# Two more block tiles for each feed-forward, with the norm's row multiplied in after the products

## The chip, the core and the metric

The kernel runs on one NeuronCore of a Trainium2 chip. The metric is the device time of one launch in microseconds (us), the median of several runs. The engines that matter are TensorE (PE, matmuls and, beside them, weight loads), VectorE (DVE), ScalarE (ACT), GpSimd (POOL, here a queue for DMAs that add into DRAM) and SyncE (SP, the queue that loads weights). Each engine executes its instructions in the order in which they were issued to it; an instruction that waits for another engine holds up everything behind it on its own engine.

## The reference

Two layers of a streaming encoder: 512 tokens, 1024 channels, float32. Each layer is a mixer and then a gated feed-forward with a causal convolution; the change lies in the feed-forwards alone.

```python
D_FF = ((8 * D_MODEL // 3 + 127) // 128) * 128          # 2816 = 22 tiles of 128
def rmsnorm(x, g):
    y = x32 * lax.rsqrt(jnp.mean(x32 * x32, axis=-1, keepdims=True) + EPS)
    return (y * g.astype(jnp.float32)).astype(x.dtype)
def conv_ffn(h, w_up, conv_w, conv_b, w_down):
    u, g = jnp.split(h @ w_up, 2, axis=-1)
    g = causal_dwconv(g, conv_w, conv_b)                # width 3
    return (jax.nn.silu(g) * u) @ w_down
x = x + conv_ffn(rmsnorm(x, norm_ffn_g[l]), ffn_w_up[l], ffn_conv_w[l], ffn_conv_b[l], ffn_w_down[l])
```

## The kernel before

**Layout.** Activations lie transposed: eight tiles `xT[j]` of 128 channels x 512 tokens. The factor of the norm is one number per token, the same for all channels; the kernel keeps it as a tile `norm.row` (128 x 512, all rows alike). Since it depends on the token alone, it may be multiplied in before the up-projection or on its result. The gain `g` is per channel and must be multiplied in before.

**Float32 products.** A float32 operand is split into a high and a low part (`split`, L138 to L141: ACT casts the high part, DVE subtracts for the low part), and a product is three matmuls (`mm3`, L194 to L196): high x high, high x low, low x high. So every weight tile costs a cast on ACT (`wh`, L140) and a subtraction on DVE (`wl`, L141) before PE can use it.

**The end of a mixer** (`finish`, L709). For each j the output projection `o` is added to `xT[j]` (L714), its square goes into the norm's sum (L288 on ACT, L289 on DVE), and `scaled` makes the high and low parts of x times g (L329 on ACT, L330 on DVE). The last three `o` are projected here, 24 matmuls of 512 columns each.

**The feed-forward's 22 tiles** of 128 hidden channels are made in two ways. A *plain* tile is two projections (gate, up) of 24 matmuls with 512 columns. A *block* tile handles the two projections and the two halves of the tokens as a 2 x 2 block product with seven products in place of eight: seven times 12 matmuls of 256 columns. For it, DVE forms sums of weights (L944) and the results are put together from the seven products (L890, L898 copies on ACT; L901, L910, L994 additions on DVE). The input side needs sums of x blocks too (`self.sums`, L807 and following splits); these are made once a layer.

Before, tiles 0 to 4 are plain and 5 to 21 are blocks. Plain tiles 0 to 2 use x times g, and the row is multiplied in afterwards (L774, L780). Beside them `forms` (L789) makes x times g times row, splits it into `ready` and forms the block sums from it; tiles 3 and 4 and all blocks use `ready`, so their results need no row.

**A block step** (`step`, L882) runs in an order written out by hand on PE, ACT and DVE. PE: product 1 (a11), 2 (a12), 3 (s2), 4 (s1), 5 (s3), the down products, product 6 (a22), 7 (s4). Products 1, 3, 5 and 6 accumulate in one PSUM bank `r1`, and ACT copies the bank between them: after product 1 (L898), after 3, 5 and 6 (L890). A later product into the bank cannot start before the copy of the earlier one is done. Between these, the step finishes the tile before it (`Tail`: last block, three taps of the convolution, Silu, product of gate and up, split), and prepares the weights of the tile after it (`nxt`). Outside the block steps a planner sets the order on each engine.

**The down-projection** of the first 16 hidden tiles is done in pieces beside the block tiles: a *unit* multiplies a group of k tiles with 128 output columns, ACT copies the result out of PSUM (L833), and a DMA on POOL's queue adds it into `xspill` in DRAM (L834). Two PSUM banks (`tr`) serve the units. Before, there are four groups of four k tiles, two units for each weight load.

Of the kernel before, what the change touches and what calls it, by code (L numbers as in the profile page):

```python
# [16 lines left out]
P = 128  # L17
# [37 lines left out]
def trunk(  # L55
# [632 lines left out]
    class OutProjection:  # L688
# [19 lines left out]
        def finish(self, gnames):  # L708
            logarithms()  # L709
            norm = Norm()  # L710
            acts = [[] for _ in gnames]
            for j in range(KT):
                o = self.o[j] if j in self.o else run(project(self.w, j * P, self.mixes))
                V.tensor_add(xT[j], xT[j], o)  # L714
                pin(G.dma_start(xspill[j], xT[j]))
                norm.add(xT[j])
                for a, g in zip(acts, gnames):
                    a.append(scaled(xT[j], g[:, j : j + 1]))
            return norm, acts

    class ChannelMixer:
# [9 lines left out]
        def __init__(self, l, act, norm, gain, beside):  # L731
            self.l, self.act, self.norm, self.gain, self.beside = l, act, norm, gain, beside
            self.w, self.fw, self.fb = ffn_w_up[l], col[f"fw{l}"], col[f"fb{l}"]
            self.hid, self.ready, self.down = [], [], {}
# [22 lines left out]
        def plain(self, j):  # L757
            scale = self.norm.row if j < UNSCALED else None
            act = self.act if j < UNSCALED else self.ready
            gate = project(self.w, DFF + j * P, act)  # L760
            up = project(self.w, j * P, act, "sc")
            if self.norm.row is None:
# [3 lines left out]
                scale = self.norm.row  # L766
# [3 lines left out]
            acc = sb("t", [P, S])  # L770
            src = og
            if scale is not None:
                src = sb("t", [P, S])
                V.tensor_tensor(out=src, in0=og, in1=scale, op=ALU.mult)  # L774
# [4 lines left out]
            if scale is not None:  # L779
                V.tensor_mul(acc, acc, scale)  # L780
# [5 lines left out]
        def forms(self):  # L786

            for j in range(KT):
                V.scalar_tensor_tensor(  # L789
                    xT[j], xT[j], self.gain[:, j : j + 1], self.norm.row, op0=ALU.mult, op1=ALU.mult  # L790
                )
                hi, lo = sb("u", [P, S], F32R), sb("u", [P, S], F32R)
                split(hi, lo, xT[j])
                self.ready.append((hi, lo))
                yield
            self.sums = []
            for k in range(KT // 2):
                b1, b2 = xT[k], xT[k + KT // 2]
# [18 lines left out]
        def load_down(self, q):  # L817

            g, jj = divmod(q, KT // 2)
            return load(rows(ffn_w_down[self.l], 2 * jj * P, 2 * P, GROUP * g, GROUP * (g + 1)), GROUP, 2 * P)  # L820

        def down_products(self, u):
            g, j = divmod(u, KT)
            w = self.down[u // 2]
            o = ps("tr")
            c = slice(u % 2 * P, (u % 2 + 1) * P)
            for k in range(GROUP):
                mm3(o, w[0][:, k, c], w[1][:, k, c], *self.hid[GROUP * g + k], k == 0, k == GROUP - 1)
            return j, o

        def add(self, j, o):
            t = sb("t", [P, S])
# [20 lines left out]
        def b(self, i, t):  # L853
            n = KT // 2
            return [tuple(x[:, t * H : (t + 1) * H] for x in p) for p in self.ready[i * n : (i + 1) * n]]
# [5 lines left out]
        def later(self):  # L861
# [17 lines left out]
            for part in (tail.last_block, tail.first_tap, tail.second_tap, tail.third_tap, tail.gated, tail.split):  # L879
                part()  # L880

        def step(self, j, w, nxt, tail):  # L882
# [10 lines left out]
            then(tail, "last_block", "first_tap")  # L893
# [17 lines left out]
            w.down_products(0)  # L911
            w.down_products(1)
# [5 lines left out]
            sum_products(new.pre[:, :H], r1, w.a22, 4)  # L918
            self.products(new.r3, w.s4, self.b(1, 1))
            return new, nxt  # L920

    class Forms:


        def __init__(self, mixer, j):
            self.mixer = mixer
            self.units = UNITS.get(j, (None, None))
            self.up, self.gate = mixer.load_pair(j)
            self.o = {}
            self.raw_down = {u // 2: mixer.load_down(u // 2) for u in self.units if u is not None and u % 2 == 0}  # L930
# [47 lines left out]
        def down_products(self, i):  # L978
            if self.units[i] is not None:
                self.o[i] = self.mixer.down_products(self.units[i])  # L980

        def add_down(self, i):
            if self.units[i] is not None:
                self.mixer.add(*self.o[i])

    class Tail:
# [5 lines left out]
        def last_block(self):  # L992
            c = self.up[:, H:]
            V.tensor_tensor(out=c, in0=c, in1=self.r3[:, :H], op=ALU.add)  # L994

# [18 lines left out]
    def channel_mixer(l, act, norm, gain, beside):  # L1014

        mixer = ChannelMixer(l, act, norm, gain, beside)
        forms = mixer.forms()
        run(mixer.plain(0))
        skips = -(turn[0] + 1) % 3
        for j in range(1, UNSCALED):  # L1020
            turn[0] += j <= skips
            weave(mixer.plain(j), forms, KT / (16.0 * (UNSCALED - 1)))
        until(lambda: len(mixer.ready) == KT, forms)
        mixer.buffers()
        for j in range(UNSCALED, PLAIN):
            units = UNITS.get(j, ())
            raws = {u // 2: mixer.load_down(u // 2) for u in units[::2]}
# [570 lines left out]
```

## Time and profile before

| | us |
|---|---|
| median of 3 runs | 1178.65 |
| lowest, highest | 1177.98, 1178.71 |
| span of the profiled execution (first to last instruction) | 1177.3 |
| PE busy | 1167.7 (99%) |
| DVE busy | 940.7 (80%) |
| ACT busy | 728.5 (62%) |

The profiled execution's time is known by its span alone. The stages of layer 0's feed-forward in it: the mixer's end from 253.8 us, plain tiles until about 340, block steps until about 580. Layer 1's: from 809 us, until about 894, until about 1136. In a timeline row stand the start, the duration, engine, line, operation and tiles, and in brackets the engine's idle time before the row and what ended it. A PE row's duration is modelled and overlaps the next; the distance of starts tells the rate.

### The profile page before, as it was taken

To read this page: it belongs to the slowest core of one execution; us is meant where nothing else is said; L and a number is where in the kernel's file an instruction comes from. 1 tells how busy PE (TensorE), PEld (TensorE's weight loads), DVE (VectorE), ACT (ScalarE), POOL (GpSimd) and SP (SyncE) were. 2 spreads that over 40 slices of the span, in tenths; PEclk is the share of its full clock that TensorE was granted. 3 is DMA by queue.
4 is the path that set the end of the run, shared out by engine and by line. 5 is a ranking of instruction groups with operands and counts; after the bars stand their busy time and mean duration, and the time that the engine had idled before them with its cause. 6 is when DMAs were issued, how large, how long until landed. Compare 5 with 4: busy or idle time off the path is not lost.

```text
span 1177.3 us, 18645 instructions
## 1 busy us (share of the span) xinstructions
PE 1167.7 (99%) x7005; PEld 1033.3 (88%) x7005; DVE 940.7 (80%) x1680; ACT 728.5 (62%) x1297; POOL 129.2 (11%) x222
## 2 busy tenths in 40 slices
PE   9999999999999999999999999999999999999997
PEld 9988888888889999999888888778889999999986
DVE  6777788887979888777688888897897887777755
ACT  6548677655656655666666677676565666666545
POOL 1211101000021111111020000101001011110100
PEclk9999999999999999999999999999999999999999
DMA  8645325243366766665563312335426456666551
GB/s 277 230 111 140 86 55 152 76 144 116 90 159 159 181 166 165 167 147 118 154 204 117 90 54 89 112 89 179 142 90 152 108 138 142 143 144 144 126 161 72
DMA packets 199277, 158.64 MB, mean 135 GB/s; under 512 B 8361, under 2 KB 178063, under 8 KB 199187
## 3 DMA queue, kind: packets, MB, share of 16 engines
q1 hardware_dynamic: 183026, 119.74, 34.5%
q0 software_dynamic: 15584, 36.67, 15.6%
q8 instruction: 55, 0.90, 0.3%
q10 hardware_dynamic: 576, 1.05, 0.2%
q14 instruction: 36, 0.29, 0.1%
HBM read 128.89 MB, written 32.46 MB: 137 GB/s over the span
## 4 chain that ended last, share of the span: by engine, by line
PE 95%; ACT 2%; DVE 2%; issue 0%; POOL 0%; POOLq 0%; DVEq 0%; ACTq 0%
PE pmm L194 18%; PE pmm L195 18%; PE pmm L196 18%; PE ptr L195 6%; PE ptr L194 6%; PE ptr L196 6%; PE psc L196 5%; PE psc L195 5%; PE psc L194 5%; PE psc L600 2%; PE ptr L1421 1%; PE ptr L1442 1%; PE ptr L1443 1%; PE ptr L669 0%; PE pmm L491 0%; PE pmm L470 0%
## 5 line engine op out<-in xcount | busy, mean ns | idle before, releaser
L194 PE MATMUL pmm<-u,wh 128*128 128x512 f32 (+1 forms) x968 | 333.2, 345 | 0.2 <-ACT u L140 0.2
L196 PE MATMUL pmm<-u,wl 128*128 128x512 f32 (+1 forms) x968 | 330.6, 342 | 0.0
L195 PE MATMUL pmm<-u,wh 128*128 128x512 f32 (+1 forms) x968 | 330.4, 342 | 0.0
L141 DVE TENSOR_TENSOR wl<-wr,wh 128x1024 fp32r<-128x1024 f32 (+3 forms) x172 | 199.7, 1162 | 82.4 <-ACT wh L140 80.9
L140 ACT CAST wh<-wr 128x1024 fp32r<-128x1024 f32 (+3 forms) x172 | 171.9, 1002 | 91.5 <-PE pmm L195 41.0
L196 PEld LDWEIGHTS pmm<-u,wl 128*128 128x128 f32 x968 | 181.8, 188 | 20.8
L194 PEld LDWEIGHTS pmm<-u,wh 128*128 128x128 f32 x968 | 181.8, 188 | 18.5 <-ACT u L140 1.1
L195 PEld LDWEIGHTS pmm<-u,wh 128*128 128x128 f32 x968 | 182.0, 188 | 18.1 <-DVE u L141 0.5
L194 PE MATMUL ptr<-u,wh 128*128 128x512 f32 x272 | 106.4, 391 | 0.0
L195 PE MATMUL ptr<-u,wh 128*128 128x512 f32 x272 | 106.2, 390 | 0.0
L196 PE MATMUL ptr<-u,wl 128*128 128x512 f32 x272 | 105.8, 389 | 0.0
L834 POOL DMA_DIRECT2D xspill<-t x64 | 55.5, 867 | 429.7 <-ACT t L833 417.2
L890 ACT COPY t<-pmm 128x256 f32<-128x256 f32 x102 | 38.0, 372 | 76.7 <-PE pmm L196 76.5
L141 DVE TENSOR_TENSOR u<-t,u 128x512 fp32r<-128x512 f32 (+1 forms) x94 | 54.1, 596 | 35.4 <-ACT u L140 35.4
L194 PE MATMUL pmm<-u,fh 128*128 128x256 f32 x272 | 75.4, 277 | 0.0
L194 PE MATMUL psc<-u,wh 128*128 128x256 f32 (+1 forms) x232 | 75.3, 324 | 0.0
L195 PE MATMUL pmm<-u,fh 128*128 128x256 f32 x272 | 75.2, 276 | 0.0
L196 PE MATMUL pmm<-u,fl 128*128 128x256 f32 x272 | 75.1, 276 | 0.0
L196 PE MATMUL psc<-u,wl 128*128 128x256 f32 (+1 forms) x232 | 75.1, 324 | 0.0
L195 PE MATMUL psc<-u,wh 128*128 128x256 f32 (+1 forms) x232 | 74.9, 323 | 0.0
L141 DVE TENSOR_TENSOR fl<-pt,fh 128x512 fp32r<-128x512 f32 x102 | 70.3, 689 | 5.1 <-ACT fh L140 1.4
L140 ACT CAST fh<-pt 128x512 fp32r<-128x512 f32 x102 | 62.9, 616 | 8.9 <-DVE pt L944 5.5
(352 smaller groups left out, 2495.9 us busy)
## 6 DMA issues: line engine op xcount, KB each, us to landing
wr<-in_ffn_w_up_dram SPq DMA_DIRECT2D x54, 512.0 KB, 6.1
wr<-in_ffn_w_down_dram SPq DMA_DIRECT2D x38, 512.0 KB, 5.1
pt<-in_ffn_w_up_dram SPq DMA_DIRECT2D x34, 512.0 KB, 7.7
xspill<-t POOLq DMA_DIRECT2D x64, 256.0 KB, 4.3
wr<-in_a_w_in_dram SPq DMA_DIRECT2D x20, 512.0 KB, 3.8
wr<-in_w_kv_dram SPq DMA_DIRECT2D x12, 512.0 KB, 4.1
xspill<-fh POOLq DMA_DIRECT2D x16, 256.0 KB, 2.8
xspill<-fl POOLq DMA_DIRECT2D x16, 256.0 KB, 2.9
```

The source lines that it names most:

```text
L140: high = A.copy(hi, src) if on_act else V.tensor_copy(hi, src)
L141: low = V.tensor_tensor(out=lo, in0=src, in1=f(hi), op=ALU.subtract)
L194: nc.tensor.matmul(o, lh, rh, start=first, stop=False, skip_group_check=more)
L195: nc.tensor.matmul(o, lh, rl, start=False, stop=False, skip_group_check=more)
L196: nc.tensor.matmul(o, ll, rh, start=False, stop=last, skip_group_check=more)
L600: nc.tensor.matmul(o, a, b, start=first and i == 0, stop=i == 1)
L834: G.dma_start(xspill[j], t, accum_op=ALU.add)
L890: A.copy(o, r[:, :H])
L1421: nc.tensor.transpose(tp[:, b * P : (b + 1) * P], es[T, h][:, b * P : (b + 1) * P], ident)
L1442: nc.tensor.matmul(o2[:, s * P :], w, hi_at(pts[h], s, s, TT - s), start=s == 0, stop=False)
L1443: nc.tensor.matmul(o2[:, s * P :], w, lo_at(pts[h], s, s, TT - s), start=False, stop=s == TT - 1)
```

## The change

Three things, and what follows from them:

1. **The sums of blocks come from x times g**, not from x times g times row. `forms` is gone; `block_sums` scales pairs of `xT` tiles by the gain on ACT (two copies of 128 x 512 for each of four k) and makes the sums. Three of the four are issued inside `finish`, in j = 4, 5 and 6, the fourth beside plain tile 0. The blocks use `act`, so nothing waits for the row before the products.
2. **The row is multiplied into a block tile's two results**: `scaled` (gate) and `scaled_up` (up), each one DVE multiplication of 128 x 512 for every block tile, after `last_block`. `first_tap` on ACT reads what `scaled` writes.
3. **Three plain tiles in place of five**, and 19 block tiles in place of 17. The down-projection begins with two groups of two k tiles: steps 3 and 4 have four units of two k tiles on one load, steps 5 to 8 two units of two k tiles on a half-size load, steps 9 to 20 two units of four k tiles as before. The third and fourth unit of a step stand between products 6 and 7. The copies of the units go to tiles with the tag `bias` (four buffers) in place of `t` (eight). In layer 1 two of the `bias` buffers hold the final gain (`fgb`) through the feed-forward.

```diff
-PLAIN, UNSCALED, GROUP, LAST = 5, 3, 4, 6
-UNITS = {PLAIN - 1: (0, 1, 2, 3), 5: (None, 4), 6: (None, 5), 7: (None, 6), 8: (None, 7)}
-UNITS.update((j, (2 * j - 10, 2 * j - 9)) for j in range(9, 21))
+PLAIN, LAST = 3, 6
+LOADS = [(0, 2, 0, 4), (0, 2, 4, 8)]
+LOADS += [(2, 4, 2 * i, 2 * i + 2) for i in range(4)]
+LOADS += [(4 * g, 4 * g + 4, 2 * i, 2 * i + 2) for g in (1, 2, 3) for i in range(4)]
+UNITS = {3 + i: tuple((i, j) for j in range(*LOADS[i][2:])) for i in range(len(LOADS))}
...
-        def finish(self, gnames):
+        def finish(self, mixer):
...
-                for a, g in zip(acts, gnames):
-                    a.append(scaled(xT[j], g[:, j : j + 1]))
-            return norm, acts
+                mixer.act.append(scaled(xT[j], mixer.gain[:, j : j + 1]))
+                if KT // 2 <= j < KT - 1:
+                    next(mixer.forms)
...
-        def forms(self):
-
-            for j in range(KT):
-                V.scalar_tensor_tensor(
-                    xT[j], xT[j], self.gain[:, j : j + 1], self.norm.row, op0=ALU.mult, op1=ALU.mult
-                )
-                hi, lo = sb("u", [P, S], F32R), sb("u", [P, S], F32R)
-                split(hi, lo, xT[j])
-                self.ready.append((hi, lo))
-                yield
+        def block_sums(self):
+
             self.sums = []
             for k in range(KT // 2):
-                b1, b2 = xT[k], xT[k + KT // 2]
+                b1, b2 = sb("u", [P, S]), sb("u", [P, S])
+                for t, i in ((b1, k), (b2, k + KT // 2)):
+                    A.activation(t, xT[i], AF.Copy, scale=self.gain[:, i : i + 1])
...
         def add(self, j, o):
-            t = sb("t", [P, S])
+            t = sb("bias", [P, S])
             A.copy(t, o)
             G.dma_start(xspill[j], t, accum_op=ALU.add)
...
-            then(tail, "last_block", "first_tap")
+            then(tail, "last_block", "scaled", "first_tap", "scaled_up")
             w.split_fourth()
...
-            w.down_products(0)
-            w.down_products(1)
+            w.down_products(0, 2)
             then(nxt, "split_sums", "sum_fourth")
             w.add_down(0)
             then(nxt, "split_gate")
             w.add_down(1)
             then(nxt, "split_down")
             sum_products(new.pre[:, :H], r1, w.a22, 4)
+            w.down_products(2, 4)
             self.products(new.r3, w.s4, self.b(1, 1))
+            w.add_down(2)
+            w.add_down(3)
...
+        def scaled(self):
+            V.tensor_mul(self.pre, self.pre, self.mixer.norm.row)
+
+        def scaled_up(self):
+            V.tensor_mul(self.up, self.up, self.mixer.norm.row)
...
-    def channel_mixer(l, act, norm, gain, beside):
-
-        mixer = ChannelMixer(l, act, norm, gain, beside)
-        forms = mixer.forms()
-        run(mixer.plain(0))
...
+    def channel_mixer(mixer):
+
+        weave(mixer.plain(0), mixer.forms, 0.25)
+        run(mixer.forms)
+        mixer.buffers()
...
+            run(mixer.plain(j))
```

**Where instructions move.** The first place is DVE's queue in a block step, from the last block of the tile before to the product of gate and up. `t` are work tiles, `psc` and `pmm` PSUM banks, `fl` the low part of a weight sum, `pt` the sums of weights. Before:

```order
L994 TENSOR_TENSOR t_4367<-t_4367,psc_4366 128x256
L141 TENSOR_TENSOR fl_4536<-pt_3237,fh_4535 128x512
L741 SCALAR_TENSOR_TENSOR t_4533<-t_4369,cols_799,t_4533 128x511
L741 SCALAR_TENSOR_TENSOR t_4533<-t_4369,cols_799,t_4533 128x510
L901 TENSOR_TENSOR t_4542<-t_4542,pmm_4540 128x256
L944 TENSOR_TENSOR pt_3237<-pt_3236 128x512
L944 TENSOR_TENSOR pt_3237<-pt_3237,wr_4528 128x512
L1009 TENSOR_TENSOR t_4533<-t_4367,t_4533 128x512
```

Of the change, in the same place (L988 is the last block, L991 `scaled`, L994 `scaled_up`, L743 the taps; `rb` is the row):

```order
L988 TENSOR_TENSOR t_3509<-t_3509,psc_3508 128x256
L991 TENSOR_TENSOR t_3511<-t_3511,rb_3082 128x512
L994 TENSOR_TENSOR t_3509<-t_3509,rb_3082 128x512
L143 TENSOR_TENSOR fl_3688<-pt_3135,fh_3687 128x512
L743 SCALAR_TENSOR_TENSOR t_3684<-t_3511,cols_799,t_3684 128x511
L743 SCALAR_TENSOR_TENSOR t_3684<-t_3511,cols_799,t_3684 128x510
L893 TENSOR_TENSOR t_3694<-t_3694,pmm_3692 128x256
L939 TENSOR_TENSOR pt_3135<-pt_3134 128x512
L939 TENSOR_TENSOR pt_3135<-pt_3135,wr_3678 128x512
L1009 TENSOR_TENSOR t_3684<-t_3509,t_3684 128x512
```

Two multiplications stand behind the last block, ahead of everything else of the step. ACT's queue keeps its order there: first tap, cast `fh` for product 7, copy after product 1, Silu, copy after product 3.

The second place is DVE's queue at the end of layer 1's mixer, behind the sixth addition of an output projection (j = 5). Before (`wl_9073` is the low part of the weights of the last projection, j = 7):

```order
L141 TENSOR_TENSOR wl_9073<-wr_9070,wh_9072 128x1024
L289 TENSOR_TENSOR rb_8948<-rb_8948,t_9023 128x512
L330 SCALAR_TENSOR_TENSOR u_9027<-fl_8494,cols_449,u_9026 128x512
L714 TENSOR_TENSOR fl_8496<-fl_8496,pmm_9036 128x512
L141 TENSOR_TENSOR wl_9121<-wr_9118,wh_9120 128x1024
```

Of the change (`wl_9321` is the same low part, L796 the block sums, L143 on `u` their low parts):

```order
L796 TENSOR_TENSOR t_9176<-u_9172 128x256
L796 TENSOR_TENSOR t_9177<-u_9173,u_9172 128x256
L796 TENSOR_TENSOR t_9176<-u_9173,t_9176 128x256
L291 TENSOR_TENSOR rb_9130<-rb_9130,t_9227 128x512
L796 TENSOR_TENSOR t_9177<-u_9173,t_9176 128x256
L143 TENSOR_TENSOR u_9182<-t_9176,u_9182 128x256
L143 TENSOR_TENSOR u_9185<-t_9176,u_9185 128x256
L143 TENSOR_TENSOR u_9188<-t_9177,u_9188 128x256
L715 TENSOR_TENSOR fl_8678<-fl_8678,pmm_9262 128x512
L143 TENSOR_TENSOR u_9191<-t_9177,u_9191 128x256
L332 SCALAR_TENSOR_TENSOR u_9231<-fl_8676,cols_449,u_9230 128x512
L143 TENSOR_TENSOR wl_9321<-wr_9318,wh_9320 128x1024
```

The subtraction that writes this low part stood first in the stretch and now stands twelfth, behind the block sums of k = 0, the seventh addition (L715) and the low part of x times g for j = 5 (L332).

More of the change, by code (lines that the diff above doesn't have):

```diff
@@ L757, in plain @@
         def plain(self, j):
[L758 to L761, printed above, removed]
+            gate = project(self.w, DFF + j * P, self.act)
+            up = project(self.w, j * P, self.act, "sc")
             if self.norm.row is None:
@@ L769, in plain @@
                 ou = None
[L770 to L774, printed above, removed]
+            acc, src = sb("t", [P, S]), sb("t", [P, S])
+            V.tensor_tensor(out=src, in0=og, in1=self.norm.row, op=ALU.mult)
             self.last_tap(j, acc, src)
@@ L1334, in more_rows @@
             bias_rows()
[L1336 removed]
+    mixer = ChannelMixer(0, col["gffn"][:, 0:8], more_rows)
+    outp.finish(mixer)
+    hid = channel_mixer(mixer)
     logarithms()
```

74 lines of the change are left out of this document (31 added, 43 removed).

## The prediction

> **What bounds the kernel now.** I read the page's engine shares first, then the chain that ended last, then the busy times of the stages, and last the rows of one block step.
>
> ```profile
> PE 1167.7 (99%) x7005; PEld 1033.3 (88%) x7005; DVE 940.7 (80%) x1680; ACT 728.5 (62%) x1297; POOL 129.2 (11%) x222
> PE 95%; ACT 2%; DVE 2%; issue 0%; POOL 0%; POOLq 0%; DVEq 0%; ACTq 0%
> 284.00:331.00 47.00, 47.00 (x208) 38.74 (x208) 46.86 (x83) 30.48 (x49) 0.00 (x0) 1.00 0.33 99
> 343.00:429.00 86.00, 86.00 (x649) 81.57 (x648) 72.24 (x106) 52.84 (x90) 14.87 (x22) 1.00 0.68 162
> 429.00:572.00 143.00, 143.00 (x1034) 133.97 (x1033) 113.28 (x164) 85.33 (x144) 23.28 (x30) 1.00 0.62 147
> ```
>
> PE is the bound everywhere: 95% of the chain, and in the stage rows (length, then busy time of PE, PEld, DVE, ACT, POOL, granted clock) it is busy throughout, in the plain tiles (284 to 331) as in the block steps (343 to 572). DVE is full in the plain tiles (46.86 of 47) and at 79% to 84% in the block steps. So the change is worth what it takes from PE, less any wait that it puts on PE. Rates, from starts of PE rows:
>
> ```profile
> 429.70 0.39 PE L196 MATMUL ptr<-u,wl 128*128 128x512 f32 x1
> 431.06 0.39 PE L196 MATMUL ptr<-u,wl 128*128 128x512 f32 x1
> 433.90 0.28 PE L196 MATMUL psc<-u,fl 128*128 128x256 f32 x1
> 434.01 0.28 PE L194 MATMUL pmm<-u,wh 128*128 128x256 f32 x1
> 436.73 0.28 PE L194 MATMUL pmm<-u,fh 128*128 128x256 f32 x1
> ```
>
> Six matmuls of 512 columns from 429.70 to 431.06: 0.227 us each. Twenty-four of 256 columns from 434.01 to 436.73: 0.1133 each. No row shows PE losing anything to the narrower form.
>
> **Term 1, PE's work.** A plain tile is 48 x 0.227 = 10.88 us, a block tile 84 x 0.1133 = 9.52. Two tiles a layer change form, in two layers: 4 x 1.36 = **5.44 us less**. The down-projection has the same matmuls (384 a layer), only spread otherwise. By its matmuls a step with two units of four k tiles, or four of two, lasts 9.52 + 24 x 0.227 = 14.96 us (long), one with half of that 12.24 (short: steps 5 to 8, before as after).
>
> **Term 2, the row in the block steps.** The rows of one long step, DVE, then ACT; product 1 starts at 434.01, product 3 at 436.73 and product 5 would follow at 439.45.
>
> ```profile
> 434.21 0.42 DVE L994 TENSOR_TENSOR t<-t,psc 128x256 f32<-128x256 f32 x1
> 434.68 0.69 DVE L141 TENSOR_TENSOR fl<-pt,fh 128x512 fp32r<-128x512 f32 x1
> 435.29 1.53 DVE L741 SCALAR_TENSOR_TENSOR t<-t,cols,t 128x511 f32<-128x511 f32 x2
> 438.06 0.69 DVE L944 TENSOR_TENSOR pt<-pt,wr 128x512 f32<-128x512 f32 x1
> 438.67 0.68 DVE L1009 TENSOR_TENSOR t<-t,t 128x512 f32<-128x512 f32 x1
> 433.32 0.82 ACT L748 ACTIVATE t<-t,cols 128x512 f32<-128x512 f32 x1
> 434.05 0.60 ACT L140 CAST fh<-pt 128x512 fp32r<-128x512 f32 x1
> 435.57 0.37 ACT L898 COPY t<-pmm 128x256 f32<-128x256 f32 x1 [0.92 <-PE pmm L196]
> 436.92 0.63 ACT L1006 ACTIVATE t<-t 128x512 f32<-128x512 f32 x1 [0.97 <-DVE t L741]
> 438.29 0.37 ACT L890 COPY t<-pmm 128x256 f32<-128x256 f32 x1 [0.74 <-PE pmm L196]
> 441.28 0.62 ACT L140 CAST u<-t 128x512 fp32r<-128x512 f32 x1
> 441.80 1.05 ACT L140 CAST wh<-wr 128x1024 fp32r<-128x1024 f32 x1
> ```
>
> What the reader is to see: the first tap (L748) runs at 433.32, before the step's product 1 has begun, because it needs nothing of product 7. The copy after product 1 (L898) then waits 0.92 us for PE and ends at 435.94, 0.8 us before product 3 needs it. That margin is what the change spends. `scaled` stands in DVE's queue behind the last block, which waits for product 7, and the first tap now waits for `scaled`; behind the first tap on ACT stand the cast `fh` and the copy that PE waits for.
>
> In time from product 1's start, with the rows' lengths and distances: last block 0.20, `scaled` 0.34 later (a 256-wide row lets the next start after 0.34, a 512-wide one after 0.61: 438.06 to 438.67) at 0.54 to 1.23. First tap 1.27 to 2.09. The cast 0.73 after the tap's start (433.32 to 434.05), 2.00. The copy 0.52 after that (441.28 to 441.80), 2.52 to 2.89. Product 3 was due at 2.72 and starts at 2.93: **0.2 us lost**. DVE meanwhile has done `scaled_up` by 1.84 and waits for the cast: `fl` 2.64, the taps 3.25 to 4.78. Silu 4.82, and the copy after product 3, which stands behind Silu, 0.53 later at 5.35 to 5.72. Product 5 was due at 5.44 + 0.2 and starts at 5.76: **0.1 us lost**. Together 0.32 us for every long step with a tail. In steps 4, 10 to 20 and 21 that is 13 x 0.32 = 4.2 us a layer. Both margins are a tenth or two wide, so the bounds are 0 and 0.6 for a step, 0 and 8 us a layer.
>
> The short steps are worse, since there DVE itself runs out:
>
> ```profile
> 355.19 0.42 DVE L901 TENSOR_TENSOR t<-t,pmm 128x256 f32<-128x256 f32 x1 [0.23 <-PE pmm L196]
> 360.14 0.69 DVE L141 TENSOR_TENSOR u<-t,u 128x512 fp32r<-128x512 f32 x1 [1.22 <-ACT u L140]
> 361.08 1.23 DVE L141 TENSOR_TENSOR wl<-wr,wh 128x1024 fp32r<-128x1024 f32 x1 [0.26 <-ACT wh L140]
> 366.03 0.42 DVE L994 TENSOR_TENSOR t<-t,psc 128x256 f32<-128x256 f32 x1
> 366.05 0.37 ACT L898 COPY t<-pmm 128x256 f32<-128x256 f32 x1 [0.47 <-PE pmm L196]
> 368.42 0.41 DVE L901 TENSOR_TENSOR t<-t,pmm 128x256 f32<-128x256 f32 x1
> ```
>
> From L901 to L901 of the next step, 355.19 to 368.42, DVE took 13.23 us, 1.48 of them idle: 11.75 of work, 1.14 of it a full down load. Already here it is over a short step of 12.24, and the last block (L994) comes as late as PE's end of the next product 1; before, only every other short step has a load, so DVE recovers. Now each of the four has a half load (0.6) and two multiplications (1.2): 11.75 - 1.14 + 1.8 = 12.4 us, plus the wait of 0.8 for the cast behind the first tap (1.84 to 2.64 above) and about 0.2 of small ones: 13.4 us, **1.2 us over** PE's 12.24. The first inherits a punctual DVE and pays 0.3, three pay 1.2. Step 8 prepares a full load (0.54 more), and step 9 starts with DVE 1.1 + 0.54 late and pays 1.7. Sum 5.6 us a layer; bounds 2 (DVE's work alone, without the wait) and 8.
>
> Term 2 is 4.2 + 5.6 = 9.8 a layer, **19.6 us**.
>
> **Term 3, block sums inside the mixers' end.** `forms` leaves: per layer eight multiplications, eight subtractions and eight casts in the plain tiles, where PE never waited for them: worth nothing. In `finish` each of three block sums brings eight 256-wide DVE instructions and six on ACT:
>
> ```profile
> 327.60 1.42 DVE L141 TENSOR_TENSOR u<-t,u 128x256 fp32r<-128x256 f32 x4
> 812.35 0.39 PE L194 MATMUL pmm<-u,wh 128*128 128x512 f32 x1
> 821.41 1.22 DVE L141 TENSOR_TENSOR wl<-wr,wh 128x1024 fp32r<-128x1024 f32 x1
> 823.70 1.05 ACT L140 CAST wh<-wr 128x1024 fp32r<-128x1024 f32 x1 [0.92 <-PE pmm L195]
> 257.73 0.39 PE L194 MATMUL pmm<-u,wh 128*128 128x512 f32 x1
> 268.81 0.69 DVE L714 TENSOR_TENSOR fl<-fl,pmm 128x512 f32<-128x512 f32 x1 [0.68 <-PE pmm L196]
> 269.71 1.23 DVE L141 TENSOR_TENSOR wl<-wr,wh 128x1024 fp32r<-128x1024 f32 x1 [0.22 <-ACT wh L140]
> 274.25 0.69 DVE L714 TENSOR_TENSOR fl<-fl,pmm 128x512 f32<-128x512 f32 x1 [2.05 <-PE pmm L196]
> 275.63 0.69 DVE L289 TENSOR_TENSOR rb<-rb,t 128x512 f32<-128x512 f32 x1 [0.70 <-ACT t L288]
> 276.25 0.75 DVE L330 SCALAR_TENSOR_TENSOR u<-fl,cols,u 128x512 fp32r<-128x512 f32 x1
> ```
>
> Four in 1.42 us, so a start every 0.34: 2.7 us of DVE a sum. Layer 1: the three projections start at 812.35. The third one's low weights were written at 821.41; PE wants them behind 24 + 2 + 2 + 22 + 2 matmuls, at 824.1. In the new order they stand behind the sum of k = 0 and the low part of j = 5. The latter needs ACT, which is held by the cast at 823.70 (a weight buffer that PE gives back then): cast to 824.6, one 256-wide cast (0.3), high part of j = 5 to 825.6, low part to 826.3, weights 826.3 to 827.5. PE waits **3.4 us**. The next sums delay j = 6 and 7 alike; by the same count PE waits 0.1 at the gate's weights and 1.2 for the parts of j = 7. Sum 4.7. Layer 0, where those weights stand ahead: three sums are 8.1 us of DVE before the last low part (276.25 to 277.0), one weight row (1.14) now stands behind it, the norm's sum (0.6) ahead of it, and the idle times from 264 to 277 in the rows (0.68, 0.22, 2.05, 0.70) take up 3.65: it ends 8.1 - 1.14 + 0.6 - 3.65 = 3.9 us later, at 280.9. PE's projections start at 257.73; behind 72 + 26 matmuls, at 279.9, it wants this part, and at 280.4 the low weights of the next projection, which DVE writes right after it (ready at 282.1): **1.7 us**, both waits in one. Term 3 is 6.4 us; bounds 1 (planner's order harmless, only layer 0's tail) and 9.
>
> *Weighed against the Trainium skill:* "TensorE: Matmul & The Clock Gate", Part 1, says that a PE idle for a window of about 3.4 us falls to half clock until it has been busy for as long; an estimate from that page's figure is half a window, 1.7 us more for the wait in layer 1, and a sum of 1201. No wait of that length lies inside this trace to show it.
>
> **Term 4, the rest.** The additions into DRAM take 4.3 us from issue to landing:
>
> ```profile
> xspill<-t POOLq DMA_DIRECT2D x64, 256.0 KB, 4.3
> ```
>
> In layer 0 four buffers cover that. In layer 1 two are left, so the third copy in steps 3 and 4 waits for the first one's landing, and ACT reaches the next step's first tap at about 2.0 in place of 1.27. I take 0.4 us; bounds 0 and 3. The end of each feed-forward has the tail longer by one multiplication (0.7), but PE has 20 matmuls (4.5 us) of other sums ahead of the last tile, where it had 15: nothing.
>
> **Sum:** -5.44 + 19.6 + 6.4 + 0.4 = **+21.0 us** on a span of 1177.3. What lies around the span (1178.65 - 1177.3 = 1.35) stays, so the median becomes 1199.6; I say 1200.
>
> **Rivals.** *The gain alone.* If copies and casts keep their margins, as the stage rows (PE busy all the time) would suggest, and the sums hide in DVE's idle time: 1178.65 - 5.4 = 1173. Against it: the queue order puts the copy PE needs behind the row. 8%. *Short steps and mixers' ends only.* The margins in long steps are 0.2 and 0.1; if handovers run a little faster than I count, 2 x 4.2 falls away: 1191. 14%. *Only the mixers' ends.* If DVE's lateness in block steps does not reach PE, 6.4 + 0.4 stand against 5.44: 1180, about level. 5%. *Clock.* In the program's last window the granted clock fell when PE had ended:
>
> ```profile
> 1170.00:1177.00 7.00, 0.64 (x6) 0.44 (x4) 2.40 (x9) 2.01 (x6) 0.00 (x0) 0.83 0.41 150
> ```
>
> A mean of 0.83 over 7 us is 1.2 us of clock lost after 0.64 of work. If the wait in layer 1 sets this off, as much again is lost when PE resumes, and a little in every step that follows late: 1201 to 1203. 7%.
>
> **From cases to numbers.** Forecast 66%, own range 1190 to 1208. The range for 8 in 10 takes in the second rival and most of the bounds: 1185 to 1209. A difference under 0.2% (2.4 us) cannot be told from none. Faster 8%, same 5%, slower 87%.
>
> **What would show it.** PE rows of product 3 that wait for ACT's copy (the line of L890 in the new numbering) and of product 5 for L882, 0.1 to 0.3 us in each long step; short steps of 13.4 between L893 rows; DVE near 100% there; PE waiting for `wl` at the end of layer 1's mixer for about 3 us. If long steps keep 15.0 and short ones 12.3, term 2 is wrong and the time falls towards 1180 or below.

## The result: slower by 2.9%, beyond the range

The changed kernel takes 1212.79 us (median; 1210.42 to 1215.12) against 1178.65 before: a ratio of 1.0287, 95% interval 1.0275 to 1.03. The forecast was 1200, with a range to 1209. The profiled execution spans 1211.2 us against 1177.3, so 33.9 us have to be found where 21.0 were forecast. One launch among the runs below, of the run with four buffers, took 2362.95 us; the ratio given there leaves it out.

The page of the changed kernel, engine shares and then the chain that ended last:

```profile
PE 1183.3 (98%) x7149; PEld 1044.9 (86%) x7149; DVE 986.1 (81%) x1768; ACT 741.4 (61%) x1345; POOL 143.1 (12%) x238
PE 74%; issue 14%; DVE 6%; ACT 4%; DMA 2%; POOL 1%; POOLq 0%; SPq 0%; ACTq 0%; DVEq 0%
```

By the shares PE is as full as before, and its busy time even grew. In the chain PE falls from 95% to 74%, DVE rises from 2% to 6%, ACT from 2% to 4%, and "issue", time in which an engine waited for nothing that the profile shows, goes from 0% to 14%. These 14% are not what the change costs: in the run below that loads the final gain later they are 2%, and it is only 4.2 us faster. The view of PE's waits names what PE waited for (total, times, longest):

```profile
PE pmm L196 <- ACT t L890: 13.0, 11, 3.1
PE pmm L198 <- DVE wl L143: 3.4, 1, 3.4
PE pmm L197 <- DVE u L332: 0.7, 2, 0.6
```

L890 is the copy after product 1, which the prediction named. The waits of the long steps from step 10 on are too short to stand in this view (it has none between 405 and 592 us); they are read from the starts of PE's rows. Now one long step, ACT's rows, then DVE's, then PE's around product 3:

```profile
489.19 0.82 ACT L750 ACTIVATE t<-t,cols 128x512 f32<-128x512 f32 x1 [1.98 <-DVE t L991]
489.91 0.61 ACT L142 CAST fh<-pt 128x512 fp32r<-128x512 f32 x1
490.42 0.36 ACT L890 COPY t<-pmm 128x256 f32<-128x256 f32 x1
493.31 0.35 ACT L882 COPY t<-pmm 128x256 f32<-128x256 f32 x1
505.95 0.36 ACT L890 COPY t<-pmm 128x256 f32<-128x256 f32 x1
488.13 0.42 DVE L988 TENSOR_TENSOR t<-t,psc 128x256 f32<-128x256 f32 x1
488.47 0.68 DVE L991 TENSOR_TENSOR t<-t,rb 128x512 f32<-128x512 f32 x1
490.54 0.28 PE L198 MATMUL pmm<-u,wl 128*128 128x256 f32 x1
490.83 0.39 PE L196 MATMUL pmm<-u,fh 128*128 128x256 f32 x1
491.06 0.28 PE L197 MATMUL pmm<-u,fh 128*128 128x256 f32 x1
492.37 0.28 PE L196 MATMUL psc<-u,wh 128*128 128x256 f32 x1
493.80 0.31 PE L196 MATMUL pmm<-u,wh 128*128 128x256 f32 x1
```

The queue order did what the prediction said: last block (488.13), row (488.47), first tap (489.19), cast, copy; the copy ends at 490.78 and PE begins product 3 at 490.83, 0.29 us after the matmul before it and so 0.18 late. But the step lasts 15.53 us (L890 to L890, 490.42 to 505.95), 0.54 more than the 14.99 of before, not 0.18 or 0.32. The rest lies behind the wait: the next matmul follows after 0.23 us in place of 0.11, and the twelve of product 4 take 1.43 us (492.37 to 493.80, 0.119 each). In the kernel before, the same twelve, and the next copy after product 1 (the one ahead of it stands in the prediction at 435.57, 14.99 us earlier):

```profile
438.09 0.28 PE L194 MATMUL psc<-u,wh 128*128 128x256 f32 x1
439.45 0.28 PE L194 MATMUL pmm<-u,wh 128*128 128x256 f32 x1
450.56 0.37 ACT L898 COPY t<-pmm 128x256 f32<-128x256 f32 x1 [0.92 <-PE pmm L196]
```

The twelve take 1.36 us, 0.1133 each. Copies L890 again: two of the first layer's short steps, then three of the second layer's first block steps, with what ACT waited for there (from the view of its waits). The last row has three short steps by stage:

```profile
356.11 0.36 ACT L890 COPY t<-pmm 128x256 f32<-128x256 f32 x1
369.71 0.36 ACT L890 COPY t<-pmm 128x256 f32<-128x256 f32 x1
898.55 0.37 ACT L890 COPY t<-pmm 128x256 f32<-128x256 f32 x1
917.18 0.37 ACT L890 COPY t<-pmm 128x256 f32<-128x256 f32 x1
932.07 0.36 ACT L890 COPY t<-pmm 128x256 f32<-128x256 f32 x1
ACT bias L822 <- DMA xspill<-bias: 5.5, 2, 3.6
352.80:393.60 40.80, 38.31 (x291) 36.15 (x290) 37.06 (x58) 24.75 (x45) 8.82 (x14) 1.00 0.79 168
```

A short step lasts 13.60 us (13.4 forecast). DVE is at 37.06 of 40.80 us in three of them (the last row, by stage), so it isn't at 100%: it waits for the late first tap. In the step of the first row PE waits 0.99 us before product 3, by its starts; the next matmul comes 0.11 late and slow ones follow, as in the long steps. In layer 1, steps 4 and 5 take 18.63 and 14.89 from copy to copy (15.5 and 13.6 in layer 0). From product 1 to product 1, by which all steps below are measured, they take 17.09 and 17.17 (16.18 and 12.80). ACT's copies of the partial sums waited 5.5 us for an addition into DRAM to free their buffer.

The whole account, from the starts of PE's matmuls against the rates of the prediction (0.1133 and 0.227 us); the column "measured" is what each place has over the same places before:

| term of the prediction | forecast | measured |
|---|---|---|
| 1: PE's work | -5.4 | -5.4 (by the count of matmuls, not measured by itself) |
| 2: long steps with a tail, 13 a layer | +8.4 | +14.5 |
| 2: short steps and step 9 | +11.2 | +12.7 |
| 3: mixers' ends, layer 0 and layer 1 | +6.4 (1.7 and 4.7) | +6.1 (1.4 and 4.7) |
| 4: buffers in layer 1, steps 3 to 5 beyond layer 0's | +0.4 | +5.5 |
| sum | +21.0 | +33.4 of 33.9 |

### The profile page after: what moved, and what is told of

Read it like the earlier page. It is cut to its first block, busy times and chain, and to the rows that moved or that the text cites. A ratio compares the mean times of both kernels' runs of the same rounds, so it can differ in the third digit from the quotient of the medians.

```text
span 1211.2 us, 19132 instructions
## 1 busy us (share of the span) xinstructions
PE 1183.3 (98%) x7149; PEld 1044.9 (86%) x7149; DVE 986.1 (81%) x1768; ACT 741.4 (61%) x1345; POOL 143.1 (12%) x238
## 4 chain that ended last, share of the span: by engine, by line
PE 74%; issue 14%; DVE 6%; ACT 4%; DMA 2%; POOL 1%; POOLq 0%; SPq 0%; ACTq 0%; DVEq 0%
PE pmm L196 15%; PE pmm L197 14%; PE pmm L198 14%; PE ptr L197 5%; PE ptr L198 5%; PE ptr L196 5%; PE psc L198 4%; PE psc L197 4%; PE psc L196 3%; PE psc L602 2%; DVE wl L143 1%; ACT wh L142 1%; DMA wr<-in_a_w_in_dram 1%; ACT t L750 1%; PE ptr L1409 1%
## 5 line engine op out<-in xcount | busy, mean ns | idle before, releaser
L143 DVE TENSOR_TENSOR wl<-wr,wh 128x1024 fp32r<-128x1024 f32 (+4 forms) x172 | 195.4, 1137 | 82.2 <-ACT wh L142 81.7
L142 ACT CAST wh<-wr 128x1024 fp32r<-128x1024 f32 (+4 forms) x172 | 168.3, 981 | 83.3 <-PE pmm L197 33.2
L823 POOL DMA_DIRECT2D xspill<-bias x80 | 69.3, 874 | 445.2 <-ACT bias L822 417.9
L143 DVE TENSOR_TENSOR fl<-pt,fh 128x512 fp32r<-128x512 f32 x114 | 78.5, 689 | 36.7 <-ACT fh L142 33.8
L196 PE MATMUL pmm<-u,fh 128*128 128x256 f32 x304 | 89.3, 294 | 13.6 <-ACT t L890 13.0
L197 PE MATMUL pmm<-u,fh 128*128 128x256 f32 x304 | 85.3, 281 | 0.0
L198 PE MATMUL pmm<-u,fl 128*128 128x256 f32 x304 | 84.9, 279 | 0.0
L750 ACT ACTIVATE t<-t,cols 128x512 f32<-128x512 f32 x44 | 35.9, 816 | 71.3 <-DVE t L991 69.3
L196 PEld LDWEIGHTS pmm<-u,fh 128*128 128x128 f32 x304 | 57.6, 189 | 23.0 <-ACT t L890 20.9
L822 ACT COPY bias<-ptr 128x512 f32<-128x512 f32 x80 | 46.9, 589 | 41.1 <-PE ptr L198 35.5
L1006 ACT ACTIVATE t<-t 128x512 f32<-128x512 f32 x38 | 24.1, 633 | 74.9 <-DVE t L743 74.9
```

The lines of the kernel that those rows point to most:

```text
L142: high = A.copy(hi, src) if on_act else V.tensor_copy(hi, src)
L143: low = V.tensor_tensor(out=lo, in0=src, in1=f(hi), op=ALU.subtract)
L196: nc.tensor.matmul(o, lh, rh, start=first, stop=False, skip_group_check=more)
L197: nc.tensor.matmul(o, lh, rl, start=False, stop=False, skip_group_check=more)
L198: nc.tensor.matmul(o, ll, rh, start=False, stop=last, skip_group_check=more)
L750: A.activation(acc, src, AF.Identity, scale=self.fw[:, 2 * FT + j : 2 * FT + j + 1], bias=self.fb[:, j : j + 1])
```

## The experiments

Times are medians. The kernel before gave 1179.12, 1178.87 and 1178.98 us beside the three groups of runs.

**Without the row in the block steps.**

```diff
-            then(tail, "last_block", "scaled", "first_tap", "scaled_up")
+            then(tail, "last_block", "first_tap")
```

> The changed kernel without the two row multiplications of a block tile (its sums then lack the norm's row; everything else stays). Theory A (the row causes nearly all that the block steps lost, and layer 1's bias buffers the rest): long steps of 15.0 us again (15.5 with the row), short steps of 12.3 (13.6), the wait of 3 us in layer 1's sixth step stays; about 1184 to 1187 us. Theory B (the late additions in layer 1 come only from engines that the row made late): that wait goes too; about 1179. Theory C (DVE's other new work, not the row, is at fault): steps stay at 15.4 and more than 13; above 1200.

Measured: 1185.48 us (ratio to before 1.0051, 1.0036 to 1.0067). The long steps are back at 15.0 (15.1 once) and the short ones at 12.27, except in layer 1, where steps 4 and 5 still last 17.35 and 16.77 us. This is theory A. The row costs 27.3 us, which is what the table has for term 2 (14.5 and 12.7), and the buffers are a matter of their own: they do not need late engines.

**The copy first.** Same work, another order on ACT:

```diff
-            then(tail, "last_block", "scaled", "first_tap", "scaled_up")
+            then(tail, "last_block", "scaled")
             w.split_fourth()
 ...
             A.copy(new.up[:, :H], r1[:, :H])
-            then(tail, "second_tap", "third_tap")
+            then(tail, "first_tap", "scaled_up", "second_tap", "third_tap")
```

> The changed kernel with the first tap, and the second multiplication, moved behind the cast of the fourth form and the copy after product 1; no work is added or left out. In a long step of the changed kernel PE waits 0.18 us before product 3, the next matmul comes 0.11 us late, and some 36 matmuls follow at 0.118 in place of 0.113 us: 0.54 us in all. Theory A (a wait empties PE's queue and all 0.54 us follow from it): long steps of 15.0, short steps of 12.6 to 12.9 (DVE's own 12.4 and small waits), 1193 to 1197 us. Theory B (the slow matmuls come from DVE's added traffic, not from the wait): long steps of 15.2 with matmuls still at 0.118, about 1204. Theory C: the first tap, now late, makes Silu and the copy after product 3 late, and PE waits before product 5 instead: no gain, 1210 or more.

Measured: 1189.44 us (1.0089, 1.0075 to 1.0103), 3.6 below theory A's range, whose gain I had summed too small. Long steps from step 10 on are at 14.99 with no slow matmul left, though DVE and ACT do exactly the same work as in the changed kernel: theory B falls. Steps 4 and 9 of layer 0 still take 15.35 and 15.92. Short steps behind the first take 12.7, with 0.28 us of wait, now before product 5. So theory C holds there, at a fraction of its size.

**The wait without the row.** The kernel before, with a copy that takes longer:

```diff
-            A.copy(new.up[:, :H], r1[:, :H])
+            for _ in range(5):
+                A.copy(new.up[:, :H], r1[:, :H])
```

> The kernel before, with the copy after product 1 done five times over (same source, same target), in all 34 block steps: it ends 1.04 us later, DVE's work stays as it was, and PE should wait 0.25 to 0.3 us before product 3. Theory A (a wait costs PE its length and about 0.35 us more, whoever caused it): 0.6 to 0.65 us a step, 1199 to 1201 us. Theory B (the slow matmuls of the changed kernel come from DVE's added work): 0.25 to 0.3 a step, 1187 to 1189, and the matmuls behind the wait at 0.113 us. If ACT has more room than counted: 1179.

Measured: 1216.82 us (1.0321, 1.0307 to 1.0335). The copies take 2 us, more than I had counted, so PE waits longer than both theories assumed; what decides is the cost beside the wait. One step, ACT and then PE:

```profile
459.42 1.99 ACT L899 COPY t<-pmm 128x256 f32<-128x256 f32 x5 [0.92 <-PE pmm L196]
460.47 0.28 PE L196 MATMUL pmm<-u,wl 128*128 128x256 f32 x1
461.47 0.39 PE L194 MATMUL pmm<-u,fh 128*128 128x256 f32 x1 [0.72 <-ACT t L899]
461.69 0.28 PE L195 MATMUL pmm<-u,fh 128*128 128x256 f32 x1
463.01 0.28 PE L194 MATMUL psc<-u,wh 128*128 128x256 f32 x1
464.31 0.28 PE L196 MATMUL psc<-u,wl 128*128 128x256 f32 x1
```

Product 3 starts 1.00 us after the matmul before it, 0.88 late. The next follows after 0.22, and from 463.01 to 464.31 eleven matmuls come at 0.118. The step lasts 16.19 us, 1.20 over the 14.99 of before: 0.88 of wait and 0.32 on top. In 8 of the 32 steps that another follows the slow matmuls are missing and the step is 0.2 us shorter. DVE is untouched here, and the surcharge is that of the changed kernel: theory A.

**Four buffers for the additions in layer 1.** The two tiles for the final gain are allocated and loaded behind the second channel mixer instead of ahead of it.

```diff
-    fgb = [sb("bias", [P, S]) for _ in range(2)]
-    for hf in range(2):
-        G.dma_start(fgb[hf], ...)
 ...
     hid = channel_mixer(mixer)
+    fgb = [sb("bias", [P, S]) for _ in range(2)]
+    for hf in range(2):
+        G.dma_start(fgb[hf], ...)
```

> The changed kernel with the two bias buffers that hold the final gain allocated and loaded behind layer 1's channel mixer, so that its additions have four buffers as in layer 0. Theory A (the copies in layer 1's first three block steps wait for a landing of 6 us because only two buffers are left): steps 3 to 5 there last as long as in layer 0 (15.0, 16.2, 12.8 in place of 15.3, 17.1, 17.2), so 5 us less: 1207 to 1208. Theory B (the landing or the late row, not the number of buffers, sets it): no change, 1212 to 1213. A loss at the end from the later load of the gain: up to 4 us more.

Measured: 1208.57 us (1.0248, 1.0234 to 1.0262), 4.2 less than the changed kernel. ACT's wait for the additions is gone, and layer 1's steps 3 to 5 last 15.03, 16.22 and 12.81 us in place of 15.29, 17.09 and 17.17, as layer 0's do: 5.5 us. Part of it was lost again in this execution at the end of layer 1's mixer, where PE ran at half its rate for a while (below).

**Block sums beside the plain tiles.**

```diff
-                if KT // 2 <= j < KT - 1:
-                    next(mixer.forms)
 ...
-        weave(mixer.plain(0), mixer.forms, 0.25)
-        run(mixer.forms)
+        weave(mixer.plain(0), mixer.forms, 4 / 48)
 ...
-            run(mixer.plain(j))
+            weave(mixer.plain(j), mixer.forms, 4 / 48)
+        run(mixer.forms)
```

> The changed kernel with no block sum inside the mixers' end: all four of a layer are spread over the three plain tiles. Theory A (term 3: the three sums inside the mixers' end cost what PE waits there, 1.4 us in layer 0 and 5.0 in layer 1, and DVE has room for them beside the plain tiles): 6 us less, 1206 to 1208. Theory B (DVE is full beside the plain tiles too, so the wait moves to the first block step): 1210 to 1214, with PE waiting for sums or for the first tiles' parts. If PE's waits of 1.0 us and less are all that matter and layer 1's wait stays: 1211.

Measured: 1220.7 us (1.0354, 1.0339 to 1.037), 8 slower than the changed kernel and worse than theory B's range. The mixers' ends have no wait left, but the last sums came behind the third plain tile, and PE waited 6.5 and 4.8 us in the first block step and then ran some 27 matmuls at half rate. The stages of layer 0, plain tiles and then that step:

```profile
282.00:296.00 14.00, 14.00 (x64) 11.58 (x63) 11.39 (x18) 9.91 (x15) 0.00 (x0) 1.00 0.37 111
296.00:306.60 10.60, 10.60 (x48) 8.78 (x47) 10.60 (x22) 7.57 (x15) 0.00 (x0) 1.00 0.18 52
306.60:316.00 9.40, 3.07 (x26) 2.87 (x25) 9.40 (x20) 6.85 (x13) 0.00 (x0) 0.94 0.36 106
```

DVE had 2.6 us free in the first 14 and none later. Four sums of 2.7 us do not fit there, so where they stand matters, and my spacing was a poor one.

**The three edits together**, and then **Silu behind the copy after product 3** as well (Silu leaves `third_tap` and becomes a part of its own):

```diff
             sum_products(new.up[:, H:], r1, w.s2, 2)
+            then(tail, "silu")
```

> The changed kernel with the three edits together: first tap behind the copy after product 1, the final gain loaded later, the sums beside the plain tiles. Theory A (the losses are separate and add up): the run with the copy first gave 1189.4; its layer 1 still lost 6.3 us in steps 3 to 5 that the two bias buffers should give back, and 6 come from the mixers' ends: 1177 to 1179, level with the kernel before. Theory B (one wait hides another, or the sums meet a full DVE): 1182 to 1186.

> As the run with the three edits, and Silu behind the copy after product 3 on ACT. Theory A (in the short steps PE waits 0.28 us before product 5 because that copy stands behind Silu): those waits and what follows them go, 0.4 to 0.5 us in six steps and 0.9 in two: 4 to 5 us less than with the three edits, 1173 to 1175. Theory B (DVE alone, full in the short steps with 12.65 us, sets them): 0 to 1 us less, and the wait stands at another place (before product 3, or at the low weights).

Measured: 1194.59 us (1.0133, 1.0116 to 1.015) and 1189.92 (1.0092, 1.0077 to 1.0107). Both totals miss, since both carry the misplaced sums: in the second the first block steps lose 9.3 and 7.9 us. The difference between them, 4.7 us, is theory A of the second: with Silu behind the copy all other steps last 15.0 and 12.27 us. DVE, at 36.21 us of 37.00 in three short steps, is full but no bound.

**The second multiplication on GpSimd**, with the edits of the run before:

```diff
-            V.tensor_mul(self.up, self.up, self.mixer.norm.row)
+            G.tensor_mul(self.up, self.up, self.mixer.norm.row)
```

> As the run with Silu later, and the second multiplication of a block tile on GpSimd in place of DVE. DVE has 0.6 us less in each step; GpSimd has no such row so far, its result is wanted some 4 us later. Theory A (DVE's work bounds the short steps): short steps of 12.27, so up to 3 us less than the run before: 1172 to 1174. Theory B (GpSimd is slow or slows DVE): more than 4 us for the multiplication, or DVE's rows longer: 1176 or more.

Measured: 1194.39 us (1.0133, 1.0118 to 1.0148), 4.5 slower than on DVE: theory B. GpSimd's multiplications in all block steps, and DVE's second (511 wide) and third tap in four short ones (groups by shape: count, busy time, mean ns of one, idle time before):

```profile
L993 POOL TENSOR_TENSOR t<-t,rb 128x512 f32<-128x512 f32 x38 | 68.3, 1796 | 61.0 <-DVE t L987 61.0
L741 DVE SCALAR_TENSOR_TENSOR t<-t,cols,t 128x511 f32<-128x511 f32 x4 | 6.0, 1509 | 1.7 <-ACT t L748 1.7
L741 DVE SCALAR_TENSOR_TENSOR t<-t,cols,t 128x510 f32<-128x510 f32 x4 | 3.0, 750 | 0.1
```

1.80 us against 0.68 on DVE, and the tap that meets it takes 1.51 us, where the third tap, and the same tap in the run before, take 0.75. What DVE saves it loses again, and more: its busy time rises from 985.3 to 997.8 us.

**The steps mended, the sums left where the change put them, then one projection later, then with wider casts, then with one sum less.** All four have the copy first, Silu later and the gain later. The edits of the sums:

```diff
-                if KT // 2 <= j < KT - 1:      # the change, and "steps only"
+                if j > KT // 2:                # one projection later
+                if j > KT // 2 + 1:            # two sums there, the rest beside plain tile 0
 ...
-                    for h in (t[:, :H], t[:, H:]):
-                        both = sb("u", [P, S], F32R)
-                        split(both[:, :H], both[:, H:], h)
+                    hi, lo = sb("u", [P, S], F32R), sb("u", [P, S], F32R)
+                    split(hi, lo, t)           # the wider casts, in the last two
```

> The changed kernel with the first tap behind the copy after product 1, Silu behind the copy after product 3, and the final gain loaded later; the block sums stay inside the mixers' end. Theory A (all that the block steps lost comes from the order on ACT and the two buffers): every step at 15.0 or 12.3, and what is left is 5.4 less for PE's work and 6.3 more for PE's waits at the mixers' ends: 1178 to 1181. Theory B (the steps were short in the run with sums beside the plain tiles only because PE had waited 6.5 us before them): short steps above 12.6, 1183 or more.

> As the run with the steps mended alone, and the three block sums of the mixers' end each one projection later (behind j = 5, 6, 7 in place of 4, 5, 6). Theory A (PE waits there because a sum stands on DVE ahead of the weights and parts it needs; 2.7 us a sum): one sum fewer ahead of the last parts, so 2 to 4 us less in the two layers together, as DVE had 2.6 us idle in the first 14 us of the plain tiles: 1175 to 1178. Theory B (DVE is as full behind as ahead, so the wait only moves): 1179 to 1182.

> As the run before, with the four casts and four low parts of a block sum, each 256 wide, made two and two of 512: 0.14 us of DVE and 0.06 of ACT less a sum by their distances (0.34 against 0.61). Theory A (DVE's work sets the waits): 0.5 to 1 us less than the run before. Theory B: the same within 0.5.

> As the run before with one block sum more taken out of the mixers' end (two there, behind j = 6 and 7; two beside plain tile 0). Theory A (DVE's idle time in the plain tiles, 2.6 us in the first 14 and little behind, takes up one sum more but no second): within 1 us of the run before. Theory B (the plain tiles are full): PE waits in the first block step, 1 to 3 us more a layer, 1180 or above.

Measured, in this order: 1180.45 us (1.0013, 1.0004 to 1.0021), 1179.67 (1.0008, 0.9999 to 1.0017), 1180.35 (1.0009, 1.0 to 1.0018) and **1175.68** (0.9972, 0.9962 to 0.9983). The first settles the block steps: every one is at 15.0 or 12.27 us, with the row in it and DVE doing its two multiplications. The second and third are level with it within their intervals: one projection later gave nothing that can be told. By PE's starts, in the second the loss at the mixers' ends only moved, to 5.0 us in layer 0 and about 2 in layer 1, where "steps only" has 1.3 and 6.3: theory B. The last one beats both kernels, by 0.28% the one before, and is 4.7 us under the run before it, outside both theories. PE's longest waits in "steps only" and in the last one:

```profile
PE pmm L198 <- DVE wl L143: 3.4, 1, 3.4
PE pmm L196 <- ACT wh L142: 1.4, 1, 1.4
```

By PE's starts, the stretch from the mixer's end to the first block step loses 1.3 and 6.3 us (layer 0, layer 1) in "steps only", 0.6 and 1.7 in the last. There 5.4 less work and 2.3 of waits make -3.1; the span says -2.7 (1174.6 against 1177.3).

## Why the prediction was right and wrong

**Right: the sign and the mechanisms.** Product 3 waits for the copy behind the first tap, short steps are slow, PE waits 3.4 us for the low weights at layer 1's mixer (3.5 late by the starts, 3.4 forecast). Term 3 came out within 0.3 of 6.4, though in layer 0 PE waited twice (0.44 and 0.57 us, each with a late matmul behind it), where the prediction had both in one wait of 1.7. Term 1 was not measured by itself; the last experiment's sum closes with it to half a microsecond.

**Wrong: the price of a wait (term 2, long steps, +6.1 us).** "Together 0.32 us for every long step with a tail" adds 0.2 and 0.1 of waits and prices a wait at its length. The wait before product 3 was 0.18, as forecast, and the wait before product 5 did not come: the copy behind Silu (493.31) was in time. What the prediction lacked is what follows a wait: 0.11 us at the second matmul and up to 0.28 us of matmuls at 0.118 to 0.119 until the 512-wide products. 11 steps a layer thus cost 0.5 to 0.6. That this belongs to the wait, not to the row, is shown twice: the copy-first order removes it with the same work, and the late copy makes it without DVE's. Why PE goes on more slowly behind a wait stays open. The "issue" of the chain does not tell: it is 1% with the late copy, where the slow matmuls follow in 24 of 32 steps, and 13% with the copy first, where the long steps from step 10 on have none (chains of the two, in this order).

```profile
PE 90%; ACT 7%; DVE 2%; issue 1%; POOL 0%; POOLq 0%; DVEq 0%; ACTq 0%
PE 74%; issue 13%; DVE 7%; ACT 4%; POOL 1%; DMA 1%; POOLq 0%; ACTq 0%; DVEq 0%
```

Step 4 was a second miss of this term: DVE was late there, and it cost 1.2 in layer 0.

**Wrong: term 4 (+5.1 us), the largest error in one place.** "I take 0.4 us; bounds 0 and 3" let the third copy wait for a landing of 4.3 us. That was the median of all additions before; now the median is 5.7, and in the steps in question

```profile
DMA to landing us min/median/max: 4.0/6.2/7.7
915.47 0.59 ACT L822 COPY bias<-ptr 128x512 f32<-128x512 f32 x1 [3.61 <-DMA xspill<-bias]
915.96 0.82 ACT L750 ACTIVATE t<-t,cols 128x512 f32<-128x512 f32 x1
914.20:917.60 3.40, 0.31 (x3) 0.11 (x1) 0.29 (x1) 2.08 (x4) 0.85 (x1) 0.93 1.11 298
917.60:920.60 3.00, 3.00 (x14) 3.00 (x15) 2.93 (x6) 0.66 (x2) 0.00 (x0) 0.51 0.88 166
```

up to 7.7 (first row; then the copy that waited and the first tap behind it; the last two are stages with length, busy times, clock, DMA share and GB/s). The stage with the longest wait moved 298 GB/s; that the other transfers there made the additions late is likely, but no run shows it. It was the fourth copy that waited, in two steps, not the third, and it stands right ahead of the first tap on ACT. The second wait was long enough to slow the clock, which the bound of 3 did not hold either.

**Short steps (+1.5 us)** had the right cause in part: the prediction called them bound by DVE. With the two copies out of the way DVE does the same work in 12.27 (12.4 by the prediction's count), so the coupling through ACT was the bound. The forecast's 13.4 came near 13.6 by counting the same wait for the tap. In part that is luck: it had 1.2 us of DVE's lateness a step, where PE waited 0.99 and lost 0.34 behind the wait.

**The rivals.** The gain alone, and the two that drop a part of term 2 or of it all, are ruled out by the steps. The clock rival, 1201 to 1203, has its mechanism but not its place. In the changed kernel's profiled execution PE stood for 3.4 us at layer 1's mixer and went on at full clock; in step 5 it stood for 3.1 and went on at 0.51 (the last row above) for 3 us, about 1.4 us lost. The Trainium skill ("TensorE: Matmul & The Clock Gate", Part 1) has the clock go by windows of about 3.4 us that run freely. The next comparison agrees with the free running: the same wait at the same place, in the changed kernel and in "steps only".

```profile
836.50:840.20 3.70, 0.36 (x2) 0.00 (x0) 3.46 (x7) 3.48 (x6) 0.54 (x1) 1.00 0.19 71
840.20:843.20 3.00, 2.99 (x13) 2.46 (x14) 3.00 (x9) 2.14 (x6) 0.00 (x0) 1.00 0.54 161
825.70:831.40 5.70, 5.70 (x13) 4.45 (x14) 5.70 (x14) 3.67 (x8) 0.00 (x0) 0.50 0.32 92
835.24:838.65 3.41, 1.62 (x8) 1.00 (x6) 3.17 (x8) 3.02 (x6) 0.54 (x1) 1.00 0.20 77
838.65:842.07 3.42, 1.86 (x8) 1.54 (x9) 3.42 (x8) 2.45 (x6) 0.00 (x0) 1.00 0.32 112
821.18:824.59 3.41, 1.17 (x6) 0.63 (x4) 3.17 (x8) 3.02 (x6) 0.54 (x1) 1.00 0.16 62
```

Full clock behind it in the one (840.20), half clock for 5.7 us in the other (825.70), 2.6 us lost. The traces show the grid itself. In every one of this case the granted clock changes only at whole multiples of 3.413 us from its first change in the trace: in the changed kernel after 911.36 us, which is 267 of them, and 3.41 later, in "steps only" after 819.20, which is 240, and 6.83 later. The last three rows are cut by that grid. In the changed kernel the wait is split over two intervals, with 1.62 and 1.86 us of PE in them; in "steps only" one interval has 1.17 us of PE, and half clock begins at its end, 824.59. The run with four buffers had the same slow stretch there, so 4.2 us came of its 5.5. The last version has no such stretch in its profile (mean clock 0.999 against 0.996 in "steps only"); the run before it has one of 3.41 us, up to 1.7 us lost. This probably is why it gained more than its sums.

## What to carry to other kernels

Price a wait on a full TensorE at its length plus a restart, here 0.3 us more before narrow matmuls, and a wait near 3 us at another one to three, since it can halve the clock; here that went by how the wait lay on a grid of 3.413 us. Before adding work to an engine off the critical path, write down what stands behind it on every queue that it passes through: here the work itself cost nothing once the copies that free PE's accumulators stood ahead of it on ACT. Take a buffer's turnaround from the transfers that run at that place, not from the median of the program.

## What the runs showed of the hardware that was not expected

- After a wait of 0.18 or 0.88 us alike, the second matmul came 0.11 us late and 256-wide matmuls followed at 0.118 in place of 0.1133 us, until wider ones came. In 8 of 32 steps of the late-copy run the slow pace was absent; why stays open.
- The clock also halved with less than a whole interval of rest. In the run with the sums one projection later, PE was busy for 1.84 of 3.41 us, with several short waits, and then ran at 0.50 (first two rows). This is more than the 1.62 us that the changed kernel had above without a fall, so the busy time of PE's rows, whose ends are modelled, does not decide it alone; what does stays open.
- Half clock lasted one interval where PE was busy for 2.97 us of it (changed kernel, third row), and two where it was busy for 2.31 of the first ("steps only", last row).

```profile
278.98:282.39 3.41, 1.84 (x6) 0.93 (x7) 3.27 (x8) 3.41 (x8) 0.06 (x1) 1.00 0.53 96
282.39:285.81 3.42, 3.42 (x10) 2.67 (x9) 1.15 (x3) 0.90 (x2) 0.51 (x1) 0.50 0.55 158
917.16:920.57 3.41, 2.97 (x14) 2.97 (x15) 3.19 (x6) 1.02 (x4) 0.04 (x1) 0.50 0.93 177
824.59:828.01 3.42, 2.31 (x6) 1.83 (x7) 3.42 (x8) 2.33 (x7) 0.00 (x0) 0.50 0.44 140
```

- A GpSimd multiplication of 128x512 f32 took 1.80 us and doubled the time of the DVE instruction that met it (1.51 against 0.75). The Trainium skill ("SBUF — State Buffer", Who interferes with whom) names a port pair that the two share and lock; the rows agree with that.
